# Third part's x and C by seven products, head 0 loaded amid the quads, and a new order at the heads' ends and at SwiGLU's front

## The chip, the cores and the metric

The kernel runs on one core of one Trainium2 chip. Its time is the device time of one execution in microseconds (us). Runs of one kernel differ by about 0.1%: the three runs of before lie between 1023.2 and 1024.15 us. All matrix work is done in fp32 through three products of operands split into a high and a low part, so TensorE (PE) does three matmuls for each product of the reference.

## The reference, cut to what matters

One encoder layer on 512 tokens of width 1024 with 4 heads (query and key width 256, value width 512) and a SwiGLU layer of width 2816:

```python
h    = rmsnorm(x, g_mix)
proj = h @ w_in
xc, gb, gc, q, k, v, g_sw, gate_a, gate_r = split(proj)
u    = gc * xc
y_a  = (gb * dwconv3(u)) @ w_a_out                      # mixer A
ret  = retention(q, k, v)                               # mixer B, both directions
y_r  = (groupnorm_per_head(ret) * swish(g_sw)) @ w_r_out
m    = sigmoid(gate_a) * y_a + sigmoid(gate_r) * y_r
x    = x + m @ w_o
x    = x + swiglu(rmsnorm(x, g_ffn))
y    = rmsnorm(x, g_final)
```

## The kernel before, in words

**Units.** Every weight goes through the core in units of 128x1024 numbers. SyncE (SP) loads a raw unit, ScalarE (ACT) casts it to its high part (L202, names `whi<-raw`), VectorE (DVE) subtracts that for the low part (L203, `wlo<-raw,whi`), and PE multiplies high by high, high by low and low by high. `plan()` lists all units in the order of their use, raw loads go out four steps of the plan ahead, and two units are kept split ahead.

**Two ways to multiply.** A plain block (`feature_major`, L341 to L343) takes 48 matmuls of 512 columns for 256 output features. A quad (`fm_quad` with `prod`, L382; `strassen` with `prod_tm`, L426) makes two such pairs of results, for two column blocks and two halves of the tokens, from 7 products of quarter matrices where the plain way has 8. In `fm_quad` one product is 24 matmuls of 256 columns. Four of the seven weight operands (t1 to t4) are sums of quarters. For most quads DVE adds them (L300). For the quads in the list `SUMMED` they are made in DRAM by copying and accumulating DMAs that GpSimd (POOL) issues (`sum_step`, L264 to L273), one step behind a store or a pow that is named for it.

**Mixer A.** Its 1024 features are done in four parts of 256: for each x, then C (multiplied into u, then the 3-tap convolution on ACT and DVE, L776 and L778), then B (multiplied in, L818 or L845), then the result's forms z are split and stored to DRAM through POOL's queue (`z_forms`). Before, x and C of the parts 0 and 1 are two quads, B of both is a third one, and the parts 2 and 3 are plain blocks (`do_mix(2)`, `do_mix(3)`).

**The heads.** The main sequence after the projection is: `mix_quads()`, `load_head(0)` (query, key, value, gate, decay table), `do_scores(0)` (24 matmuls of 512 columns; their eviction is L872, then hi and lo), `split_v`, `do_mix(2)`. Then for each head: load the next head, `do_pv` (48 matmuls; for each of four token blocks statistics L893 to L895 on DVE, a pow on POOL L896, a multiply on DVE L899, a scaling on ACT L901), scores of the next head, `do_t` (16 transposes on DVE, L217), and a piece of other work for PE behind which these hide: `do_mix(3)` for head 0, the W_r product of the head before (`do_wr`, its sums on DVE are L933) for the others.

**SwiGLU's front.** The last products of m @ W_o add into y (`join`, L1021). `complete` squares a finished half row on ACT (L1026), scales and sums on DVE (L1028, L1031), takes the pow on POOL (L1033) and normalizes on DVE (L1036). `tr_o` transposes the result on PE (L1049), and splits it (ACT L1052, DVE L1054) beside an fp32 copy on ACT (L1053). From these come four forms s1 to s4 (DVE L1002, then split by L202 and L203) that SwiGLU's first quad needs for its second, third, fifth and seventh product. While they are made, PE runs the first products of other quads (`first_tokens`).

The pools that this touches: 14 tiles of 1 MB, 5 units each of high and low parts, 9 tiles of 128x512, 10 raw tiles, 8 banks of PSUM.

Of the kernel before, what the change touches and what calls it, by code (L numbers as in the profile page):

```python
# [17 lines left out]
P = 128  # L18
# [53 lines left out]

def plan():

    out = []  # L80

    def a(name, col):
        out.append(("c", name, 0, 8, col, 256))

    def b(name, row, nk, col, nc):
        out.append(("c", name, row, nk, col, nc))

    def quad(c0, c1):
# [12 lines left out]
    for c in (0, 512):  # L101
        quad(C_GA + c, C_GR + c)
    for c0, c1 in ((C_XC, C_GC), (C_XC + 256, C_GC + 256), (C_GB, C_GB + 256)):
        for name in FORMS:
            out.append(("q", ("x", c0, c1), name, 0, 4))
    for s in (2, 3):
        for c in (C_XC, C_GC, C_GB):
            a("w_in", c + s * 256)
    for h in range(HEADS):
        for c in (0, 512):  # L110
            b("w_r_out", h * VD, 4, c, 512)
    for kind, name in [("a", x) for x in FORMS[:6]] + [("o", "b11"), ("a", "b22")] + [
            ("o", x) for x in ("t1", "t2", "b21", "b22", "t3", "t4")]:
        for u in (0, 2):
            out.append(("q", (kind,), name, u, 2))
    def f(q, *names):
        for n in names:
            out.append(("q", ("f", q), n, 0, 4))

    for q, name in FIRST_PRODUCTS:  # L120
        f(q, name)
    for q0, n in FF_PARTS:
        for q in range(q0, q0 + n):
            between, behind = beside(q)
            f(q, "t1", "t2")
            if between:
                f(*between)
            f(q, "t3")
            if behind:
                f(*behind)  # L130
            f(q, "t4", "b22")
        units = [(name, u) for name in FORMS for u in range(0, n, 2)]
        if q0 + n == NQ:

            i = units.index(("b21", 2))
            units[i:i + 3] = units[i + 1:i + 3] + units[i:i + 1]
        for name, u in units:
            out.append(("q", ("d", q0), name, u, min(2, n - u)))
    return out
# [9 lines left out]
SUMMED = (("f", 0), ("f", 1), ("o",))  # L149
# [24 lines left out]
def block_kernel(ctx: ExitStack, tc: tile.TileContext, xw0, xw, xT, xtok, wpack, wquad, cols, decs, rot, g_ffn, g_final, out):  # L174
# [23 lines left out]

    def split(src, hi, lo, scale=None, round=None):

        if scale is None:
            first = (round or nc.scalar.copy)(hi, src)  # L202
            nc.vector.tensor_tensor(out=lo, in0=src, in1=hi.bitcast(F32), op=ALU.subtract)  # L203
# [18 lines left out]

    made = []
# [7 lines left out]
    def prefetch_block(loads, splits):  # L231
# [4 lines left out]
        for c in range(2):  # L236
            if loads:
                loads(c)
            nc.sync.dma_start(st[c], wpack[i][:, c * QH:(c + 1) * QH])
# [22 lines left out]
    steps = {"quads": sums_of(SUMMED[:2]), "heads": sums_of(SUMMED[2:])}  # L262
# [16 lines left out]

    def load_raws(upto):  # L280
        while loaded[0] < len(LOADS) and LOADS[loaded[0]][0] <= upto:
# [3 lines left out]
            nc.sync.dma_start(t[:, 0:n], src[:, 0:n])  # L285
            raws[quad, name, u] = t
            loaded[0] += 1
# [456 lines left out]
    def do_quad(left, right, func, func_left=None):  # L744
        def ev_sum(dst, o, f):
            def ev(tt, t):
# [3 lines left out]
                if tt and not o:  # L750
# [56 lines left out]
    def do_mix(s):  # L807
        us, c = [], bigtile()[:, 0:2, :]
        feature_major(xg, lambda m, ps: us.append(snap(ps)))
        u = u_tile()  # L810

        def ev_c(m, ps):
            nc.vector.tensor_tensor(out=u[:, m, 1:513], in0=ps, in1=us[m], op=ALU.mult)
            conv(m, 2 * s + m, u[:, m], c[:, m])
        feature_major(xg, ev_c)

        def ev_b(m, ps):
            nc.vector.tensor_tensor(out=c[:, m], in0=ps, in1=c[:, m], op=ALU.mult)  # L818
        feature_major(xg, ev_b)
        z_forms(s, c)  # L820

# [4 lines left out]

    def mix_quads():

        c = bigtile().rearrange("p (s m) t -> p s m t", s=2)
        for s in range(2):  # L830
            u, got = u_tile(), {}

            def ev21(ps):
                nc.vector.tensor_tensor(out=u[:, :, 257:513], in0=halves(ps), in1=halves(got["c2"]), op=ALU.mult)

            def ev12(t):
                nc.vector.tensor_tensor(out=u[:, :, 1:257], in0=halves(got["x1"]), in1=halves(t), op=ALU.mult)
            fm_quad(xf, lambda t: got.update(x1=t), ev21, lambda t: got.update(c2=t), ev12)
            for m in range(2):
                conv(m, 2 * s + m, u[:, m], c[:, s, m])  # L840
# [6 lines left out]
        fm_quad(xf, times(0, T1), times(0, T2), times(1, T2), times(1, T1))  # L847
        for s in range(2):
            z_forms(s, c[:, s])


    def load(src, dt=F32):
        t = bigtile(dt)
        nc.sync.dma_start(t if dt == F32 else t.bitcast(F32), src)
# [28 lines left out]
    def do_pv(p, vv, sg):  # L883

        for nb in range(NB):
# [11 lines left out]
            sum_step(power, "heads")  # L897
# [40 lines left out]
    mix_quads()  # L938
    nxt = load_head(0)
# [61 lines left out]
    def form(out, name, o, in0, in1, op):  # L1001
        nc.vector.tensor_tensor(out=o, in0=in0, in1=in1, op=op)  # L1002
        out[name] = form_tile()
        split(o, *out[name])

# [33 lines left out]
    def tr_o(nb):  # L1039
        th, o = nb // 2, (nb % 2) * P  # L1040
        if nb % 2 == 0:
            t = bigtile()
            for q in range(2):
                XF[q, th] = form_tile()
                xf32[q, th] = t[:, 2 * q:2 * q + 2, :].rearrange("p a (b c) -> p (a b) c", c=256)
        for q in range(2):
# [3 lines left out]
            ps = ps.rearrange("p (k t) -> p k t", k=4)  # L1050
            hi, lo = (t[:, :, o:o + P] for t in XF[q, th])
            nc.scalar.copy(hi, ps)  # L1052
            nc.scalar.copy(xf32[q, th][:, :, o:o + P], ps)  # L1053
            nc.vector.tensor_tensor(out=lo, in0=ps, in1=hi.bitcast(F32), op=ALU.subtract)  # L1054
# [36 lines left out]
    def ev(tt):  # L1091
        join(2 + tt, 1, a[tt], ALU.subtract)
        complete(2 + tt, 1, 0)
        if tt == 0:
            tr_o(0)
    prod_tm(4, of(M["s3"]), a, False, False, ev)

    def ev(tt):
        join(2 + tt, 0, a[tt])
        complete(2 + tt, 0, 1)  # L1100
        if tt == 0:
            tr_o(1)
# [115 lines left out]
    form(XF, "s4", a12, a12, a22, ALU.add)  # L1218
# [179 lines left out]
```

## Time and profile before

| what | before |
|---|---|
| time, median of three runs (lowest, highest) | 1023.71 us (1023.2, 1024.15) |
| the profiled execution, its own time | 1024.53 us |
| its span, first to last instruction | 1022.7 us |
| granted clock of PE | 1.000 |
| busy: POOL | 138.1 us, 14% |
| DMA: over the span | 211 GB/s |

The span leaves 1.8 us of the profiled execution's time that lie around it. A row of a timeline or of the chain of waits gives a start and a length in us, the engine, the line and the names; in brackets behind it stands how long the engine had been idle and what released it. In the groups, the number behind x is a count, then come busy us and the mean of one in ns, then the idle time ahead of them. A matmul's length in the timeline is longer than the distance to the next one's start, because matmuls overlap: the distance is what one costs.

### The profile page before, as it was taken

The page shows a single profiled execution, that of the slowest core. Times are in us where ns is not written, and L with a number is a line of the kernel's source. Part 1 is how long each engine was busy: PE and PEld are TensorE (multiplying, and loading weights), DVE is VectorE, ACT ScalarE, POOL GpSimd, SP SyncE. Part 2 cuts the span into 40 slices and gives each one's busy share as a digit, 9 for nine tenths or more (in the row PEclk, how much of TensorE's full clock was granted, in tenths as well). Part 3 has the DMA queues.
Part 4 walks back from the last instruction along what each step waited for, and adds up shares of the span by engine and source line. Part 5 has one row for each costly group of instructions (what it writes and reads, how often), then busy time and mean ns, then how long its engine had stood idle before and what let it go on. Part 6 is the DMA issues. An engine that isn't in the chain of part 4 may idle for free.

```text
span 1022.7 us, 14808 instructions
## 1 busy us (share of the span) xinstructions
PE 1012.4 (99%) x5586; PEld 882.3 (86%) x5586; DVE 902.7 (88%) x1169; ACT 548.0 (54%) x744; POOL 138.1 (14%) x221
## 2 busy tenths in 40 slices
PE   9999999999999999999999999999999999999997
PEld 7888888888888998888888788889998999899986
DVE  7878998979798988797979898999998999889996
ACT  7547656553656455342532325576654565556554
POOL 0030231222112003304021100010002000110011
PEclk9999999999999999999999999999999999999999
DMA  9525487694767657939496855573418522663433
GB/s 348 208 73 196 167 296 216 206 319 144 258 205 231 257 200 264 347 125 340 116 349 262 261 212 180 153 247 120 140 38 223 179 83 83 192 157 105 165 69 97
DMA packets 53352, 200.24 MB, mean 196 GB/s; under 512 B 7264, under 2 KB 7392, under 8 KB 48672
## 3 DMA queue, kind: packets, MB, share of 16 engines
q1 hardware_dynamic: 37600, 137.39, 38.4%
q0 software_dynamic: 15392, 61.62, 20.8%
q8 instruction: 44, 0.72, 0.3%
q10 hardware_dynamic: 288, 0.29, 0.1%
q14 instruction: 28, 0.23, 0.1%
HBM read 160.73 MB, written 55.31 MB: 211 GB/s over the span
## 4 chain that ended last, share of the span: by engine, by line
PE 41%; DVE 6%; issue 2%; POOL 1%; ACT 1%; DMA 0%; POOLq 0%; DVEq 0%
PE bank L382 21%; PE bank L426 17%; DVE big L217 2%; PE bank L341 1%; DVE big L933 1%; PE bank L342 1%; PE bank L343 1%; DVE wlo L203 1%; DVE big L206 0%; DVE big L203 0%; PE bank L994 0%; POOL bnmv L896 0%; DMA raw<-wquad 0%; PE bank L1049 0%; DVE bnst L893 0%
## 5 line engine op out<-in xcount | busy, mean ns | idle before, releaser
L202 ACT CAST whi<-raw 128x1024 fp32r<-128x1024 f32 (+2 forms) x299 | 302.7, 1028 | 256.6 <-PE bank L426 62.2
L203 DVE TENSOR_TENSOR wlo<-raw,whi 128x1024 fp32r<-128x1024 f32 (+2 forms) x300 | 352.2, 1190 | 64.3 <-ACT whi L202 63.8
L382 PE MATMUL bank<-xform,whi 128*128 128x256 f32 x1424 | 257.8, 283 | 0.9 <-DVE xform L203 0.6
L382 PEld LDWEIGHTS bank<-xform,whi 128*128 128x128 f32 x1424 | 222.1, 192 | 2.2 <-DVE xform L203 0.8
L382 PE MATMUL bank<-xform,wlo 128*128 128x256 f32 x712 | 201.1, 283 | 0.4 <-DVE wlo L203 0.4
L426 PE MATMUL bank<-whi,big 128*128 128x512 f32 x596 | 187.5, 390 | 0.0
L426 PE MATMUL bank<-whi,xform 128*128 128x512 f32 x496 | 157.1, 390 | 0.0
L300 DVE TENSOR_TENSOR raw<-raw 128x1024 f32<-128x1024 f32 (+1 forms) x128 | 151.7, 1201 | 4.9 <-DMA raw<-wquad 4.0
L382 PEld LDWEIGHTS bank<-xform,wlo 128*128 128x128 f32 x712 | 136.4, 192 | 0.6 <-DVE wlo L203 0.6
L426 PEld LDWEIGHTS bank<-whi,big 128*128 128x128 f32 x596 | 111.9, 188 | 24.0 <-ACT t L433 0.4
L426 PE MATMUL bank<-wlo,big 128*128 128x512 f32 x298 | 116.0, 389 | 0.0
L426 PEld LDWEIGHTS bank<-whi,xform 128*128 128x128 f32 x496 | 92.9, 188 | 19.7 <-DVE xform L203 0.6
L426 PE MATMUL bank<-wlo,xform 128*128 128x512 f32 x248 | 96.5, 389 | 0.0
L433 ACT COPY t<-bank 128x512 f32<-128x512 f32 x105 | 61.1, 586 | 56.0 <-PE bank L382 29.7
L341 PE MATMUL bank<-big,whi 128*128 128x512 f32 x220 | 85.7, 390 | 0.0
L343 PE MATMUL bank<-big,wlo 128*128 128x512 f32 x220 | 85.6, 389 | 0.0
L342 PE MATMUL bank<-big,whi 128*128 128x512 f32 x220 | 85.6, 389 | 0.0
L426 PEld LDWEIGHTS bank<-wlo,big 128*128 128x128 f32 x298 | 55.9, 188 | 11.4
L426 PEld LDWEIGHTS bank<-wlo,xform 128*128 128x128 f32 x248 | 46.6, 188 | 9.6
L341 PE MATMUL bank<-whi,big 128*128 128x512 f32 x128 | 49.9, 390 | 1.2 <-DVE big L933 1.2
L342 PE MATMUL bank<-wlo,big 128*128 128x512 f32 x128 | 49.8, 389 | 0.0
L343 PE MATMUL bank<-whi,big 128*128 128x512 f32 x128 | 49.8, 389 | 0.0
(202 smaller groups left out, 1375.1 us busy)
## 6 DMA issues: line engine op xcount, KB each, us to landing
raw<-wquad SPq DMA_DIRECT2D x140, 512.0 KB, 4.9
raw<-wpack SPq DMA_DIRECT2D x42, 512.0 KB, 5.8
t_f<-wquad POOLq DMA_DIRECT2D x12, 512.0 KB, 6.4
z<-t POOLq DMA_DIRECT2D x24, 256.0 KB, 4.5
t_o<-wquad POOLq DMA_DIRECT2D x12, 512.0 KB, 7.8
zform<-z POOLq DMA_DIRECT2D x6, 1024.0 KB, 7.1
v<-t POOLq DMA_DIRECT2D x16, 256.0 KB, 5.5
sg<-t POOLq DMA_DIRECT2D x16, 256.0 KB, 4.9
```

Source lines behind the costliest of these rows:

```text
L202: first = (round or nc.scalar.copy)(hi, src)
L203: nc.vector.tensor_tensor(out=lo, in0=src, in1=hi.bitcast(F32), op=ALU.subtract)
L217: nc.vector.transpose(o[:, :, :, b, :], i[:, :, :, q, :])
L300: nc.vector.tensor_tensor(out=t, in0=t, in1=raws[quad, more, u][:, 0:n], op=ALU.add)
L341: nc.tensor.matmul(ps, lh, rh, start=first, stop=False)
L342: nc.tensor.matmul(ps, lh, rl, start=False, stop=False)
L343: nc.tensor.matmul(ps, ll, rh, start=False, stop=last)
L382: nc.tensor.matmul(o, l[:, c], r[:, k], start=start and s == 0 and k == 0 and i == 0, stop=stop and k == 3 and i == 2, skip_group_check=True)
L426: nc.tensor.matmul(pss[tt], l, r[:, c], start=start and k == 0 and i == 0, stop=stop and k == n - 1 and i == 2, skip_group_check=True)
L433: nc.scalar.copy(t, ps)
L933: nc.vector.tensor_tensor(out=t, in0=ps, in1=t, op=ALU.add)
```

## The change

Five edits, whose line numbers in the rows below are those of the changed kernel where they stand after the word "now":

1. The third part's x and C become a third quad, `xc_quad(2)`, ahead of B's quad. Its sums are made in DRAM (it heads the list `SUMMED`), with eight more DMAs of POOL, so that all 24 steps "quads" are spread over twice as many stores as before. `do_mix(2)` keeps B alone, 48 matmuls. The plan loses two plain blocks (4 units) and gains 7 units.
2. Query, key, value and gate of head 0 are loaded by SP amid the raw loads from the second quad on, one behind every third of them. The decay table follows B's quad. Loads of plain blocks after that stand behind the last head load.
3. In `do_pv`, the four DMAs of the steps "heads" stand behind the head's last pow, not one behind each.
4. `complete`: the factor 1/D moves into the Square, the addition of EPS to POOL, the last sum to ACT. `tr_o`: both transposes first, then hi and lo, and the fp32 copies behind the last lo. `tr_o(0)` is called after the twelfth matmul of its place rather than amid them, and `tr_o(1)` ahead of the last twelve matmuls of W_o.
5. SwiGLU's front: form s2 follows s1 at once, and each further form stands behind the split of the one before.

```diff
+XC = ("x", C_XC + 512, C_GC + 512)
...
-    for c0, c1 in ((C_XC, C_GC), (C_XC + 256, C_GC + 256), (C_GB, C_GB + 256)):
+    for c0, c1 in ((C_XC, C_GC), (C_XC + 256, C_GC + 256), XC[1:], (C_GB, C_GB + 256)):
...
-        for c in (C_XC, C_GC, C_GB):
+        for c in (C_GB,) if s == 2 else (C_XC, C_GC, C_GB):
...
-SUMMED = (("f", 0), ("f", 1), ("o",))
+SUMMED = (XC, ("f", 0), ("f", 1), ("o",))
...
-                if tt and not o:
+                if tt:
                     sum_step(last)
...
     def mix_quads():
...
+        xc_quad(0, c[:, 0])
+        head = []
+        for src, dt in ((qkd[0][0], F32R), (qkd[0][1], F32R), (vd[0], F32), (sgd[0], F32)):
+            among.append(lambda src=src, dt=dt: head.append(load(src, dt)))
+        xc_quad(1, c[:, 1])
+        part2.append(bigtile()[:, 0:2, :])
+        xc_quad(2, part2[0])
...
             power = nc.gpsimd.tensor_tensor(out=mv[:, 3:4], in0=mv[:, 2:3], in1=mhalf[:, 0:1], op=ALU.pow)
-            sum_step(power, "heads")
+            if nb == NB - 1:
+
+                for _ in range(4):
+                    sum_step(power, "heads")
...
-        nc.scalar.activation(t512(), yt, AF.Square, accum_out=ac[:, last:last + 1])
+        nc.scalar.activation(t512(), yt, AF.Square, scale=D ** -0.5, accum_out=ac[:, last:last + 1])
         if not last:
-            nc.vector.tensor_scalar(out=ac[:, 3:4], in0=ac[:, 0:1], scalar1=1.0 / D, scalar2=EPS,
-                                    op0=ALU.mult, op1=ALU.add)
+            nc.gpsimd.tensor_scalar_add(ac[:, 3:4], ac[:, 0:1], EPS)
             return
-        nc.vector.scalar_tensor_tensor(out=ac[:, 4:5], in0=ac[:, 1:2], scalar=1.0 / D,
-                                       in1=ac[:, 3:4], op0=ALU.mult, op1=ALU.add)
+        nc.scalar.activation(ac[:, 4:5], ac[:, 1:2], AF.Identity, bias=ac[:, 3:4])
...
     form(XF, "s1", a22, a21, a22, ALU.subtract)
+    low = form(XF, "s2", a22, a22, a11, ALU.subtract)
     first_tokens(*FIRST_PRODUCTS[2])
-    form(XF, "s2", a22, a22, a11, ALU.subtract)
     first_tokens(*FIRST_PRODUCTS[3])
-    form(XF, "s3", a21, a11, a21, ALU.subtract)
+    with tc.issue_after(low.ins):
+        low = form(XF, "s3", a21, a11, a21, ALU.subtract)
```

Three places where the rows of an engine change. The first is DVE between the scores of head 0 and `do_pv(0)`. Before (t512_3608 is the last block of scores, big_3567 the low part of the scores, big_3613 that of v, in two halves, and u_3685 the product of C and x):

```order
L872 SCALAR_TENSOR_TENSOR t512_3608<-bank_3601,tab_3556 128x512
L203 TENSOR_TENSOR big_3567<-t512_3597,big_3566 128x512
L203 TENSOR_TENSOR big_3613<-big_3562,big_3612 128x1024
L203 TENSOR_TENSOR big_3567<-t512_3608,big_3566 128x512
L203 TENSOR_TENSOR big_3613<-big_3562,big_3612 128x1024
L203 TENSOR_TENSOR wlo_3697<-raw_3689,whi_3696 128x1024
L203 TENSOR_TENSOR wlo_3763<-raw_3758,whi_3762 128x1024
L813 TENSOR_TENSOR u_3685<-bank_3700,t512_3656 128x512
```

Now the same steps (big_3859 is the low part of v), with the multiplications by B (L884) straight behind them:

```order
L911 SCALAR_TENSOR_TENSOR t512_3854<-bank_3847,tab_3750 128x512
L210 TENSOR_TENSOR big_3813<-t512_3843,big_3812 128x512
L210 TENSOR_TENSOR big_3859<-big_3337,big_3858 128x1024
L210 TENSOR_TENSOR big_3813<-t512_3854,big_3812 128x512
L210 TENSOR_TENSOR big_3859<-big_3337,big_3858 128x1024
L884 TENSOR_TENSOR big_3296<-bank_3876,big_3296 128x512
L884 TENSOR_TENSOR big_3296<-bank_3902,big_3296 128x512
L210 TENSOR_TENSOR wlo_4145<-raw_4137,whi_4144 128x1024
```

DVE's own steps up to v's low part stand as before; what has gone is the work with x and C behind it, and on PE the matmuls between the scores and `do_pv(0)` fall from 144 to 48.

The second place is POOL at the end of head 2. Before, pows and DMAs (t2 is the sum in DRAM, first copied from t1, then added to) alternate:

```order
L896 TENSOR_TENSOR bnmv_4602<-bnmv_4602,mhalf_188 128x1
L273 DMA t2_0_o_90<-t1_0_o_89 16x8192
L896 TENSOR_TENSOR bnmv_4624<-bnmv_4624,mhalf_188 128x1
L273 DMA t2_2_o_94<-t1_2_o_93 16x8192
L896 TENSOR_TENSOR bnmv_4646<-bnmv_4646,mhalf_188 128x1
L271 DMA t2_0_o_90<-wquad 64x2048
L896 TENSOR_TENSOR bnmv_4668<-bnmv_4668,mhalf_188 128x1
L271 DMA t2_2_o_94<-wquad 64x2048
```

Now the four pows come first:

```order
L935 TENSOR_TENSOR bnmv_4708<-bnmv_4708,mhalf_192 128x1
L935 TENSOR_TENSOR bnmv_4729<-bnmv_4729,mhalf_192 128x1
L935 TENSOR_TENSOR bnmv_4750<-bnmv_4750,mhalf_192 128x1
L935 TENSOR_TENSOR bnmv_4771<-bnmv_4771,mhalf_192 128x1
L283 DMA t2_0_o_94<-t1_0_o_93 16x8192
L283 DMA t2_2_o_98<-t1_2_o_97 16x8192
L281 DMA t2_0_o_94<-wquad 64x2048
L281 DMA t2_2_o_98<-wquad 64x2048
```

No pow has a DMA ahead of it any more, in head 2 and likewise in head 3.

The third place is DVE at SwiGLU's front. Before, the forms (L1002, in the order s1 to s4) come ahead of the low parts of s2, s3 and s4 (the last three xform rows):

```order
L1002 TENSOR_TENSOR big_6089<-big_6089 128x1024
L203 TENSOR_TENSOR wlo_6200<-raw_5990,whi_6199 128x1024
L1002 TENSOR_TENSOR big_6089<-big_5948,big_6089 128x1024
L203 TENSOR_TENSOR xform_6157<-big_6089,xform_6157 128x1024
L1163 TENSOR_TENSOR t512_6191<-bank_6203,t512_6191 128x512
L1002 TENSOR_TENSOR big_6089<-big_6089,big_5948 128x1024
L203 TENSOR_TENSOR wlo_6236<-raw_6056,whi_6235 128x1024
L1002 TENSOR_TENSOR big_5948<-big_5948,big_6089 128x1024
L203 TENSOR_TENSOR xform_6194<-big_6089,xform_6194 128x1024
L203 TENSOR_TENSOR xform_6230<-big_6089,xform_6230 128x1024
L203 TENSOR_TENSOR xform_6267<-big_5948,xform_6267 128x1024
L203 TENSOR_TENSOR wlo_6274<-raw_6108,whi_6273 128x1024
```

Now each form (L1043) is followed by its own low part and by weight units:

```order
L1043 TENSOR_TENSOR big_6195<-big_6195 128x1024
L1205 TENSOR_TENSOR t512_6301<-bank_6309,t512_6301 128x512
L210 TENSOR_TENSOR wlo_6410<-raw_6270,whi_6409 128x1024
L210 TENSOR_TENSOR xform_6263<-big_6195,xform_6263 128x1024
L1043 TENSOR_TENSOR big_6195<-big_6195,big_6067 128x1024
L210 TENSOR_TENSOR wlo_6442<-raw_6303,whi_6441 128x1024
L210 TENSOR_TENSOR xform_6267<-big_6195,xform_6267 128x1024
L1043 TENSOR_TENSOR big_6195<-big_6067,big_6195 128x1024
L210 TENSOR_TENSOR wlo_6474<-raw_6339,whi_6473 128x1024
L210 TENSOR_TENSOR xform_6336<-big_6195,xform_6336 128x1024
L1043 TENSOR_TENSOR big_6067<-big_6067,big_6195 128x1024
```

The low parts of s1 and s2 move ahead of the forms s3 and s4, and a weight unit stands between every two forms.

More of the change, by code (lines that the diff above doesn't have):

```diff
@@ L1 @@
-from contextlib import ExitStack
+from contextlib import ExitStack, nullcontext
 import numpy as np
@@ L202, in split @@
             first = (round or nc.scalar.copy)(hi, src)
[L203 removed]
+            low_of[0] = nc.vector.tensor_tensor(out=lo, in0=src, in1=hi.bitcast(F32), op=ALU.subtract)
         else:
@@ L221, in block_kernel @@
     block = [0]
+    behind = []
     made = []
@@ L238, in prefetch_block @@
                 loads(c)
-            nc.sync.dma_start(st[c], wpack[i][:, c * QH:(c + 1) * QH])
+            with tc.issue_after(behind[-1].ins) if behind else nullcontext():
+                nc.sync.dma_start(st[c], wpack[i][:, c * QH:(c + 1) * QH])
         for c in range(2):
@@ L284, in load_raws @@
             src = wsum[quad, name, u] if name[0] == "t" else quarter(quad, name, u)
-            nc.sync.dma_start(t[:, 0:n], src[:, 0:n])
+            raw = nc.sync.dma_start(t[:, 0:n], src[:, 0:n])
             raws[quad, name, u] = t
+            if among and loaded[0] % 3 == 0:
+                with tc.issue_after(raw.ins):
+                    among.pop(0)()
             loaded[0] += 1
@@ L847, in mix_quads, with do_mix, ev_c, ev_b @@
         fm_quad(xf, times(0, T1), times(0, T2), times(1, T2), times(1, T1))
+        while among:
+            among.pop(0)()
+        tab = misctile(896, "tab")
+        nc.sync.dma_start(tab, tabs[0])
         for s in range(2):
             z_forms(s, c[:, s])
+        behind.append(last[-1])
+        return head[0:2], tab, *head[2:]
+    def do_mix(s):
+        if s == 2:
+            c = part2[0]
+        else:
+            us, c = [], bigtile()[:, 0:2, :]
+            feature_major(xg, lambda m, ps: us.append(snap(ps)))
+            u = u_tile()
+            def ev_c(m, ps):
+                nc.vector.tensor_tensor(out=u[:, m, 1:513], in0=ps, in1=us[m], op=ALU.mult)
+                conv(m, 2 * s + m, u[:, m], c[:, m])
+            feature_major(xg, ev_c)
+        def ev_b(m, ps):
+            nc.vector.tensor_tensor(out=c[:, m], in0=ps, in1=c[:, m], op=ALU.mult)
+        feature_major(xg, ev_b)
+        z_forms(s, c)
+    last = []
     def load(src, dt=F32):
         t = bigtile(dt)
-        nc.sync.dma_start(t if dt == F32 else t.bitcast(F32), src)
+        last.append(nc.sync.dma_start(t if dt == F32 else t.bitcast(F32), src))
         return t
@@ L1049, in tr_o @@
                 nc.tensor.transpose(ps[:, k * P:(k + 1) * P], hs[nb][q][:, k * P:(k + 1) * P], ident)
[L1050 to L1054, printed above, removed]
+            pss.append(ps.rearrange("p (k t) -> p k t", k=4))
+            last = split(pss[q], *(t[:, :, o:o + P] for t in XF[q, th]))
+        with tc.issue_after(last.ins):
+            for q in range(2):
+                nc.scalar.copy(xf32[q, th][:, :, o:o + P], pss[q])
     po = {}
```

51 lines of the change are left out of this document (22 added, 29 removed).

## The prediction

> **What bounds the kernel now.** I read the page first, for the engine that is full:
>
> ```profile
> PE 1012.4 (99%) x5586; PEld 882.3 (86%) x5586; DVE 902.7 (88%) x1169; ACT 548.0 (54%) x744; POOL 138.1 (14%) x221
> ```
>
> PE is busy for 99% of the span at a granted clock of 1.000, so time goes down by fewer or cheaper matmuls, or by the few places where PE waits. The list of PE's waits names those, with total, count and longest:
>
> ```profile
> PE bank L476 <- DVE t L473: 1.4, 1, 1.4
> PE bank L341 <- DVE big L933: 1.2, 1, 1.2
> PE bank L382 <- DVE xform L203: 0.6, 1, 0.6
> PE bank L382 <- DVE wlo L203: 0.4, 1, 0.4
> PE bank L1049 <- DVE t L1036: 0.3, 1, 0.3
> PE bank L382 <- ACT xform L1052: 0.2, 1, 0.2
> ```
>
> The first is the program's start, which the change leaves. The second is the end of the heads, the other four lie at SwiGLU's front. Together these five are 2.7 us, and as matmuls' starts show below they cost some 4.0. What a matmul costs is read from two undisturbed stretches of the chain of waits (start, length, count):
>
> ```profile
> 602.77 27.20 PE bank L426 x120
> ...
> 709.23 48.73 PE bank L382 x404
> ```
>
> 512 columns cost 27.20/120 = 0.2267 us, 256 columns 48.73/404 = 0.1206 us, a little over half (0.1134).
>
> **The products.** The third part's x and C lose 2 x 48 matmuls of 512 columns, 96 x 0.2267 = 21.76 us, and gain 7 x 24 of 256 columns, 168 x 0.1206 = 20.26 us. PE is full on both sides, so this is -1.5 us. One product in eight is saved, 2.7 us at equal price per column; the shorter matmuls take 1.2 back. The Trainium skill, page "TensorE: Matmul & The Clock Gate", section "Back-to-back issue gap", gives for an isolated matmul N/2.4 + 2.5 ns; by that estimate the edit would bring 20.7 - 18.3 = 2.4 us. The same section gives 131 ns for 512 columns in a stream; by that the 96 old matmuls would take only 12.6 us and the edit would lose. The trace's 0.2267 us in a stream of 120 speaks against the second figure, and its 0.1206 is above the first, so neither enters the sum.
>
> The quad's weights cost DVE 7 subtractions where 4 were, and its evictions a few more; that falls into the stretch before 400 us, where DVE's busy time (third column behind the window: PE, PEld, DVE) stays under PE's:
>
> ```profile
> 360.00:380.00 20.00, 20.00 (x161) 19.42 (x160) 17.47 (x22) 11.30 (x14) 0.03 (x1) 1.00 0.48 172
> 380.00:400.00 20.00, 20.00 (x110) 17.44 (x109) 17.44 (x32) 9.05 (x14) 10.50 (x16) 1.00 0.87 310
> 400.00:420.00 20.00, 20.00 (x90) 16.53 (x89) 12.77 (x18) 7.98 (x11) 0.00 (x0) 1.00 0.79 298
> ...
> 460.00:480.00 20.00, 20.00 (x90) 16.57 (x89) 13.45 (x22) 5.57 (x8) 4.81 (x7) 1.00 0.94 354
> ```
>
> Its four sums come from DRAM, so no L300 additions join. I cost this at nothing; without that cover it would be some 4 us.
>
> **A new wait at head 0's P times V.** Before, DVE splits v behind the scores while PE has 144 matmuls of `do_mix(2)` to do; now there are 48. The scores end where the first matmul from whi starts, and v's low part is the pair of 128x1024 subtractions:
>
> ```profile
> 388.72 0.39 PE L343 MATMUL bank<-big 128*128 128x512 f32 x1
> 388.94 0.39 PE L341 MATMUL bank<-big,whi 128*128 128x512 f32 x1
> ```
> ```profile
> 392.73 0.69 DVE L203 TENSOR_TENSOR t<-t,t 128x512 fp32r<-128x512 f32 x1 [0.82 <-DMA z<-t]
> 394.80 0.69 DVE L203 TENSOR_TENSOR t<-t,t 128x512 fp32r<-128x512 f32 x1 [1.39 <-DMA z<-t]
> ...
> 399.94 1.22 DVE L203 TENSOR_TENSOR big<-big 128x1024 fp32r<-128x1024 f32 x1
> ...
> 401.68 1.22 DVE L203 TENSOR_TENSOR big<-big 128x1024 fp32r<-128x1024 f32 x1
> 402.82 2.36 DVE L203 TENSOR_TENSOR wlo<-raw,whi 128x1024 fp32r<-128x1024 f32 x2
> ```
>
> PE would be through B at 388.94 + 48 x 0.2267 = 399.8. The second matmul of P times V needs v's first low half, done at 401.1 (start plus length), so PE waits some 1.2 us; its eighth needs the second half, done at 402.9, which gives another 0.3. Sum +1.5 us. DVE's order up to there is unchanged, and so is what delays it: two waits, 2.2 us, for z stores to land and free their tiles. If other loads move out of z's way, v is ready at 398.9 and the cost is 0; if they double, it is 3.7. I take 1.5, the rows as they stand. DVE's work with B and z, now bunched behind it, runs out in the loose 460 to 480 window (13.45 of 20).
>
> **The heads' ends.** POOL runs its queue in order. At head 3 the last variance was ready at 561.96, but POOL stood before a DMA that waited for another to land:
>
> ```profile
> 561.81 0.15 DVE L895 TENSOR_SCALAR bnmv<-bnmv 128x1 f32<-128x1 f32 x1
> ...
> 565.97 11.45 DVE L217 STREAM_TRANSPOSE big<-big 32x512 f32<-32x512 f32 x16 [3.34 <-ACT big L901]
> ...
> 581.30 1.28 DVE L933 TENSOR_TENSOR big<-bank,big 128x512 f32<-128x512 f32 x2
> ```
> ```profile
> 563.72 0.86 POOL L271 DMA_DIRECT2D t_o<-wquad  x1 [2.77 <-DMA t_o<-t_o]
> 564.32 0.86 POOL L896 TENSOR_TENSOR bnmv<-bnmv,mhalf 128x1 f32<-128x1 f32 x1
> ```
> ```profile
> 580.48 0.39 PE L343 MATMUL bank<-whi,big 128*128 128x512 f32 x1
> 582.04 0.50 PE L341 MATMUL bank<-whi,big 128*128 128x512 f32 x1 [1.17 <-DVE big L933]
> ```
>
> With the pow first, it starts 564.32 - 561.96 = 2.4 us earlier, and so do the 16 transposes and the sums that release PE. PE's shortfall is 582.04 - 580.48 - 0.23 = 1.33, and 0.1 on the next matmul; it goes as a whole, with 0.9 us to spare: -1.4. The lower end is -1.0, if the transposes gain less than that. The four DMAs now wait behind the pow, POOL alone holds them, and the next things in its queue are form loads that waited for PE until 579.8 anyway. The Trainium skill, page "DMA: Bandwidth & Descriptors", section "Anatomy of one DMA", says that a DMA's wait is done by the issuing sequencer ahead of dispatch; the row of 2.77 us agrees. It also prices a DMA at 2.0 us plus bytes at 436 GB/s, an estimate of 3.2 us for these 512 KB, by which the pow would hardly have waited; the page of the profile has more than twice that, and the sum goes by it:
>
> ```profile
> t_f<-wquad POOLq DMA_DIRECT2D x12, 512.0 KB, 6.4
> z<-t POOLq DMA_DIRECT2D x24, 256.0 KB, 4.5
> t_o<-wquad POOLq DMA_DIRECT2D x12, 512.0 KB, 7.8
> ```
>
> The quad's own eight sums use this queue too. Its last four follow one another where f's came two and two, so a DMA can wait up to 6.4 us less the distance to the one before, and stores to DRAM stand behind it. At the spacing of the stores there that is 0 to 4 us of POOL, which PE sees only if the nine t512 tiles run out: 0, at most 0.5.
>
> **SwiGLU's front.** PE's rows there, each with the one ahead of it:
>
> ```profile
> 676.03 0.39 PE L426 MATMUL bank<-wlo,xform 128*128 128x512 f32 x1
> 676.76 0.63 PE L1049 MATMUL bank<-ident,t 128*128 128x128 f32 x4 [0.34 <-DVE t L1036]
> ...
> 681.32 1.03 PE L1049 MATMUL bank<-ident,t 128*128 128x128 f32 x8
> 682.60 0.39 PE L382 MATMUL bank<-xform,whi 128*128 128x256 f32 x1 [0.24 <-ACT xform L1052]
> ...
> 704.44 0.76 PE L382 MATMUL bank<-xform,whi 128*128 128x256 f32 x5
> 705.83 0.39 PE L382 MATMUL bank<-xform,whi 128*128 128x256 f32 x1 [0.63 <-DVE xform L203]
> ...
> 708.56 0.28 PE L382 MATMUL bank<-xform,wlo 128*128 128x256 f32 x1
> 709.23 0.39 PE L382 MATMUL bank<-xform,wlo 128*128 128x256 f32 x1 [0.39 <-DVE wlo L203]
> ```
>
> Against the steady distances the shortfalls are 0.5 (676.76 - 676.03 - 0.23), 0.5 (682.60 less eight transposes of 0.11, and 0.1 on the next), 0.9 (705.83 less five times 0.12, and 0.1) and 0.65: 2.55 in all. The first two get cover: `tr_o(0)` moves behind four more matmuls (0.9 us), and twelve (2.7 us) follow `tr_o(1)`. The third is s2's low part, which stood behind two forms, s3 and s4, and now stands ahead of them. The fourth is a weight unit behind three low parts in a row, now spread out. DVE's work itself barely falls, so I leave 0.35 of the last: -2.2, between -2.55 and -1.0. EPS on POOL is used only once the second half row is squared, so its price is hidden.
>
> **The sum.** -1.5 + 1.5 - 1.4 - 2.2 = -3.6 us on the profiled execution's 1024.53, which is 1020.9. That execution lies 0.8 above the median of 1023.71; from the median the forecast is 1020.1. All terms at their good ends give -5.5 (1018.2), all at their bad ends -1.5 + 3.7 - 1.0 - 1.0 + 0.5 = +0.7 (1024.4).
>
> **The rivals.** *Nothing new waits, all named waits go*: z's stores land in time and v is ready. For it speaks that the two waits hang on the DMA engines alone (share 0.87 between 380 and 400), where loads run beside z's stores; against it, the order of these loads hardly changes. 1018.2.
>
> *DVE is the bound at the front.* There it works 19.27 of 20 us:
>
> ```profile
> 680.00:700.00 20.00, 19.76 (x151) 18.75 (x150) 19.27 (x29) 16.97 (x30) 2.00 (x2) 1.00 0.50 156
> ```
>
> A PE that arrives 1 us earlier then finds the next unit 1 us late, and only 0.5 of the 2.55 is kept: -1.5 + 1.5 - 1.4 - 0.5 = -1.9, 1021.8. Against it: behind 709.23 PE did not wait again, though four units stood in a row.
>
> *Slower: z's stores hold up head 0.* DVE reaches v only behind two waits for z stores. If these land in 7.8 us, as POOL's accumulating transfers do, and not in 4.5, each wait grows by 3.3 and P times V waits 1.5 + 6.6 = 8.1 us: -1.5 + 8.1 - 1.4 - 2.2 = +3.0, 1026.7. It turns slower by over 0.2% once they need over 7.3 us. Against it: the same stores go out at the same point with no more traffic beside them.
>
> *The seven products are not cheaper*, if the shorter matmuls cost what the 512 do per column and 0.03 us more: 168 x 0.143 = 24, which gives +2.3 in place of -1.5, 1023.9. The x404 row excludes it almost wholly.
>
> **How the numbers follow.** Forecast 0.50, all waits gone 0.17, DVE's bound 0.20, slower through z 0.12, no cheaper products 0.01. About 0.2%, 2.05 us, is what a measurement can tell from no change: faster means under 1021.7, slower over 1025.8. So faster is 0.50 + 0.17 = 0.67, the same 0.20 + 0.01 = 0.21, slower 0.12. The range, 1018.2 to 1024.4, is that of the terms' ends; it leaves out the slower case and some of the tails.
>
> **What would show it.** Right: seven groups of L382-like matmuls more, 168 in 20.3 us; one PE wait of 1 to 1.5 us on DVE's split of v behind B's 48 matmuls; no wait on L933's successor near 577; pow rows at head 3 without a DMA between; the four front waits gone or one small. Wrong: a PE wait of over 4 us at head 0, waits at the front that kept their sum under other names, or a new wait in the quads of 100 to 300 us behind POOL's stores.

## The result, and the profile after

The changed kernel takes 1031.86 us (median of 6 runs, 1030.32 to 1032.42) where the kernel before took 1023.93 beside it (6 runs, 1023.2 to 1025.63): ratio 1.007, 95% interval 1.006 to 1.008. It is slower by 7.9 us. The profiled execution took 1031.72 us with a span of 1029.9 and a mean granted clock of PE of 0.995, not 1.000.

The list of PE's waits after (total, count, longest):

```profile
PE bank L356 <- ACT big L209: 4.3, 1, 4.3
PE bank L357 <- DVE big L210: 2.1, 1, 2.1
PE bank L1090 <- DVE t L1076: 1.6, 1, 1.6
PE bank L491 <- DVE t L488: 1.4, 1, 1.4
```

The waits at head 3 (1.2) and at SwiGLU's forms (0.6 and 0.4) have gone. In their place stand two at head 0's P times V, 6.4 us together, and one of 1.6 ahead of the transposes at SwiGLU's front. The quads themselves came out near what was worked out; the chain of waits has 26 of their products, of 24 matmuls each, in a row:

```profile
323.48 75.65 PE bank L397 x624
```

That is 75.65/624 = 0.1212 us for a matmul of 256 columns, with the short delays at the starts of some products included.

**Head 0.** PE's timeline from the end of B's 48 matmuls:

```profile
421.06 0.39 PE L358 MATMUL bank<-big,wlo 128*128 128x512 f32 x1
425.72 0.59 PE L356 MATMUL bank<-big 128*128 128x512 f32 x1 [4.27 <-ACT big L209]
428.40 0.80 PE L357 MATMUL bank<-big 128*128 128x512 f32 x1 [2.09 <-DVE big L210]
428.99 0.63 PE L358 MATMUL bank<-big 128*128 128x512 f32 x1
429.41 0.63 PE L356 MATMUL bank<-big 128*128 128x512 f32 x1
...
432.82 0.40 PE L358 MATMUL bank<-big 128*128 128x512 f32 x1
```

Beyond the steady 0.227 us from start to start, the first two gaps are 4.4 and 2.45 us. After them PE goes on at 0.43 us a matmul, about half speed, until 432.8: another 2.2 us. Sum 9.1. The table of windows shows the granted clock there (the third number from the end):

```profile
420.00:440.00 20.00, 13.64 (x50) 10.48 (x49) 17.32 (x32) 8.23 (x12) 7.48 (x12) 0.83 0.85 316
```

What PE waited for is on DVE, the rows that answer to the two waits for z stores of before (0.82 and 1.39 us):

```profile
414.05 0.69 DVE L210 TENSOR_TENSOR t<-t,t 128x512 fp32r<-128x512 f32 x1 [0.96 <-DMA z<-t]
420.07 0.69 DVE L210 TENSOR_TENSOR t<-t,t 128x512 fp32r<-128x512 f32 x1 [5.33 <-DMA z<-t]
421.30 0.43 DVE L210 TENSOR_TENSOR t<-big,t 128x256 fp32r<-128x256 f32 x1 [0.53 <-DMA z<-t]
421.64 0.68 DVE L911 SCALAR_TENSOR_TENSOR t<-bank,tab 128x512 f32<-128x512 f32 x1
423.38 1.43 DVE L911 SCALAR_TENSOR_TENSOR t<-bank,tab 128x512 f32<-128x512 f32 x2 [1.05 <-DMA z<-t]
...
427.12 1.22 DVE L210 TENSOR_TENSOR big<-big 128x1024 fp32r<-128x1024 f32 x1
```

Now they are four waits with 7.9 us, and the scores (L911) and the split of v (the last row) stand behind them. The DMA issues from 400 to 425 us say which transfers ran together (KB, median us from issue to landing):

```profile
z<-t POOLq DMA_DIRECT2D x12, 256.0 KB, 8.0
...
big<-qh SPq DMA_DIRECT2D x1, 1024.0 KB, 9.0
big<-ql SPq DMA_DIRECT2D x1, 1024.0 KB, 12.0
big<-v SPq DMA_DIRECT2D x1, 1024.0 KB, 8.0
```

The same view of before, from 380 to 400 us:

```profile
z<-t POOLq DMA_DIRECT2D x12, 256.0 KB, 4.4
```

The z stores take nearly twice as long. The four of 256 KB that go out between 410.4 and 414.9 us take 11.0 us to land; three that go out ahead of them, between 400 and 408, take 5.2. Between the two groups lie the loads of query and key of head 1 (qh holds their high parts, ql the low parts). SP's timeline of the changed kernel has them at 410.62, 4 us after the end of B's quad at 406.5; in the kernel before they stand at 405.75, 21 us after its end at 385.1. The value of head 1 follows only at 421.75, when DVE's longest wait is over:

```profile
410.62 0.33 SPq L893 DMA_DIRECT2D big<-qh  x1
411.11 0.33 SPq L893 DMA_DIRECT2D big<-ql  x1
421.75 0.32 SPq L893 DMA_DIRECT2D big<-v  x1
```
```profile
405.75 0.33 SPq L854 DMA_DIRECT2D big<-qh  x1
```

**SwiGLU's front.** PE's timeline at the new wait:

```profile
694.45 0.28 PE L397 MATMUL bank<-xform,wlo 128*128 128x256 f32 x1
696.34 1.38 PE L1090 MATMUL bank<-ident,t 128*128 128x128 f32 x8 [1.61 <-DVE t L1076]
```

These are the transposes of token block 2. DVE's timeline shows why their input is late: the join of that block (L1063) stands behind the low parts of `tr_o(1)` (the xform row), 3.4 us after PE had finished its product at 688.1:

```profile
690.32 1.29 DVE L210 TENSOR_TENSOR xform<-bank,xform 128x512 fp32r<-128x512 f32 x2
691.52 1.28 DVE L1063 TENSOR_TENSOR big<-big,bank 128x512 f32<-128x512 f32 x2
...
695.53 1.41 DVE L1076 SCALAR_TENSOR_TENSOR t<-big,ac,gb 128x512 f32<-128x512 f32 x2 [0.46 <-POOL ac L1073]
```

**The sum of PE's shortfalls.** For each profile I added up how much later each matmul starts after the one before than the steady distance (0.2267 us for 512 columns, 0.120 for 256, 0.110 for a transpose), by stage. The stages with head 0 and behind are given in us of the span; for the kernel before, head 0's P times V lies at 422 and for the changed kernel at 421:

| kernel | start, to 20 | to 406 | head 0, to 445 | to 570 | to 620 | front, to 730 | rest | steady |
|---|---|---|---|---|---|---|---|---|
| before | 1.5 | 1.6 | 0.0 | 0.0 | 1.5 | 2.9 | 1.2 | 1006.1 |
| changed | 2.2 | 2.1 | 9.1 | 0.0 | 0.0 | 2.7 | 1.1 | 1004.5 |
| late_head1 | 1.9 | 1.8 | 2.7 | 0.5 | 0.0 | 2.7 | 1.0 | 1004.5 |
| z_after | 2.0 | 1.8 | 0.0 | 1.3 | 0.0 | 2.7 | 1.2 | 1004.5 |
| join_first | 1.7 | 1.8 | 8.8 | 0.0 | 0.0 | 2.0 | 1.3 | 1004.5 |
| heads_only | 2.7 | 1.6 | 0.0 | 0.0 | 0.0 | 2.9 | 1.1 | 1006.1 |
| forms_only | 2.2 | 1.6 | 0.0 | 0.0 | 1.6 | 1.6 | 1.3 | 1006.1 |
| no_xc | 1.8 | 1.6 | 0.0 | 0.0 | 0.0 | 1.6 | 1.3 | 1006.1 |
| best | 2.2 | 2.0 | 0.0 | 0.8 | 0.0 | 1.7 | 1.2 | 1004.5 |
| best2 | 2.1 | 1.9 | 0.0 | 0.9 | 0.0 | 1.9 | 3.8 | 1004.5 |

The last column is the sum of all steady distances; it follows from the number of matmuls and is not itself a measurement. From before to changed it falls by 1.6 and the shortfalls rise by 8.6, together +7.0 us; the spans differ by 7.2. The start varies by 1.2 us between executions of whatever kernel, so a single profile's time says nothing about a microsecond, but the stages do.

### The profile page after: what moved, and what is told of

Read it like the earlier page. It is cut to its first block, busy times and chain, and to the rows that moved or that the text cites. A ratio compares the mean times of both kernels' runs of the same rounds, so it can differ in the third digit from the quotient of the medians.

```text
span 1029.9 us, 14988 instructions
## 1 busy us (share of the span) xinstructions
PE 1014.1 (98%) x5658; PEld 886.4 (86%) x5658; DVE 907.3 (88%) x1167; ACT 553.3 (54%) x752; POOL 144.7 (14%) x233
## 4 chain that ended last, share of the span: by engine, by line
PE 91%; DVE 4%; DMA 1%; issue 1%; POOL 1%; ACT 1%; POOLq 0%; DVEq 0%; ACTq 0%
PE bank L441 35%; PE bank L397 29%; PE bank L357 9%; PE bank L356 9%; PE bank L358 9%; DVE wlo L210 1%; DMA z<-t 1%; DVE xform L210 1%; DVE big L1063 1%; POOL z L647 1%; DMA ydr<-big 0%; PE bank L491 0%; DVE big L1043 0%; PE bank L676 0%; DVE big L1017 0%
## 5 line engine op out<-in xcount | busy, mean ns | idle before, releaser
L209 ACT CAST whi<-raw 128x1024 fp32r<-128x1024 f32 (+2 forms) x302 | 306.2, 1029 | 265.9 <-PE bank L441 59.5
L210 DVE TENSOR_TENSOR wlo<-raw,whi 128x1024 fp32r<-128x1024 f32 (+2 forms) x303 | 356.5, 1192 | 66.8 <-ACT whi L209 66.1
L397 PE MATMUL bank<-xform,whi 128*128 128x256 f32 x1488 | 269.3, 283 | 0.0
L397 PEld LDWEIGHTS bank<-xform,whi 128*128 128x128 f32 x1488 | 232.2, 192 | 1.0 <-ACT t L448 0.5
L397 PE MATMUL bank<-xform,wlo 128*128 128x256 f32 x744 | 210.1, 283 | 0.0
L397 PEld LDWEIGHTS bank<-xform,wlo 128*128 128x128 f32 x744 | 142.6, 192 | 0.0
L356 PE MATMUL bank<-big,whi 128*128 128x512 f32 x188 | 73.3, 390 | 0.0
L358 PE MATMUL bank<-big,wlo 128*128 128x512 f32 x188 | 73.2, 389 | 0.0
L357 PE MATMUL bank<-big,whi 128*128 128x512 f32 x188 | 73.1, 389 | 0.0
```

The costliest lines, as they stand in the source:

```text
L210: low_of[0] = nc.vector.tensor_tensor(out=lo, in0=src, in1=hi.bitcast(F32), op=ALU.subtract)
L356: nc.tensor.matmul(ps, lh, rh, start=first, stop=False)
L357: nc.tensor.matmul(ps, lh, rl, start=False, stop=False)
L358: nc.tensor.matmul(ps, ll, rh, start=False, stop=last)
L397: nc.tensor.matmul(o, l[:, c], r[:, k], start=start and s == 0 and k == 0 and i == 0, stop=stop and k == 3 and i == 2, skip_group_check=True)
```

## The experiments

My theory after the result: the loads of head 1 come some 17 us earlier against B's quad than before, take the DMA engines from the z stores, and DVE cannot reach the scores of head 0 until those have landed. The rival: 48 matmuls are too short a cover and POOL's stores are slow by themselves.

**late_head1** holds the four loads of head 1 until the scores of head 0 are split.

```diff
-    def load(src, dt=F32):
+    def load(src, dt=F32, gate=None):
         t = bigtile(dt)
+        if gate is not None:
+            nc.vector.tensor_copy(t[:, 0, 0:1], gate if dt == F32R else gate.bitcast(F32))
...
-        return [load(t, F32R) for t in qkd[h]], tab, load(vd[h]), load(sgd[h])
+        gate = p[1][:, 3, 0:1] if h == 1 else None
+        return [load(t, F32R, gate) for t in qkd[h]], tab, load(vd[h], F32, gate), load(sgd[h], F32, gate)
```

> The changed kernel, with the four loads of head 1 held until the scores of head 0 are split (each load's tile first gets one column written by DVE behind that split). Theory, head 1's loads of 1 MB each collide with the z stores: the z stores land in 4 to 5 us as in the kernel before, DVE's waits for them fall from 7.9 us to 2 to 3, PE waits 1 to 2 us at P times V instead of 4.4 and 2.5, its clock stays at 1.00 there, and the time is 1023.5 to 1025.5 us. Rival, the cover of 48 matmuls is too short and POOL's stores are slow by themselves: waits and time stay within 1.5 us of the changed kernel, 1030.4 or more.

Measured: 1025.03 us beside 1024.45 for the kernel before, ratio 1.0003 (0.9994 to 1.0012), so some 7 us less than the changed kernel. PE's waits and the DMA issues from 400 to 425 us:

```profile
PE bank L1093 <- DVE t L1079: 1.6, 1, 1.6
PE bank L357 <- DVE big L210: 1.5, 1, 1.5
...
PE bank L357 <- DMA big<-ql: 0.2, 1, 0.2
```
```profile
z<-t POOLq DMA_DIRECT2D x12, 256.0 KB, 5.0
```

The theory stands: with nothing changed but the time of these loads, of what stands behind them on SP's queue, and four writes of one column on DVE behind the split, z lands in 5.0 us and not 8.0 (in 5.3 and not 11.0 for the stores sent out between 410.4 and 414.9). DVE waits 2.9 us for it and not 7.9, and PE's first gap is 1.6 us with no half-speed matmuls behind it. The rival holds for those 1.6 us, which is the cost of the short cover. Head 1 then waits a little for its own late loads (the third row).

**z_after** leaves the loads where the change puts them and calls the z forms of part 1 behind the scores and the split of v.

```diff
...
-        for s in range(2):
-            z_forms(s, c[:, s])
+        z_forms(0, c[:, 0])
+        later.append(lambda: z_forms(1, c[:, 1]))
...
     vv, sg = split_v(nxt[2]), nxt[3]
+    later.pop()()
     do_mix(2)
```

> The changed kernel, with the z forms of part 1 called behind the scores and the split of v, so that DVE need not wait for z stores before it reaches them; head 1's loads stay where the change puts them. Theory, the loads only hurt because z's waits stand ahead of the scores on DVE: P times V starts with a wait under 1 us although the z stores still land late, 1021.5 to 1024 us. Rival, DVE's own work or the late loads hold P times V anyway: a PE wait of 3 us or more stays, 1028 or more.

Measured: 1023.81 us, ratio 0.9994 (0.9985 to 1.0003). The waits at P times V are gone altogether, though the loads of head 1 still run beside z (DMA issues from 400 to 425 us):

```profile
big<-ql SPq DMA_DIRECT2D x1, 1024.0 KB, 12.5
```

So the collision costs through the order on DVE: with the scores ahead of the waits, PE is not held. The collision itself is weaker here too, as fewer stores go out together with the loads: one of 256 KB sent out between 410.4 and 414.9 still takes 9.4 us, but the median from 400 to 425 is 5.1. A part of the gain is given back. The P times V of head 2 has to wait for a bank behind the evictions of head 0's W_r product (ACT L973): two starts of PE lie 1.1 us apart, 0.9 more than the steady distance, where the kernel before has no such gap:

```profile
507.57 0.39 PE L358 MATMUL bank<-whi,big 128*128 128x512 f32 x1
508.67 0.50 PE L356 MATMUL bank<-big 128*128 128x512 f32 x1 [0.72 <-ACT big L973]
```

ACT splits the transposed result of head 1 ahead of those evictions, and PE, no longer held at head 0, catches up with them.

**join_first** undoes a part of the fourth edit: the join and the completion of W_o's last products are called ahead of `tr_o(1)`.

```diff
-        if tt == 0:
-            tr_o(1)
         join(2 + tt, 0, a[tt])
         complete(2 + tt, 0, 1)
+        if tt == 0:
+            tr_o(1)
```

> The changed kernel, with the join and completion of W_o's last products called ahead of tr_o(1) again. Theory, the wait of 1.9 us before the transposes of token block 2 comes from that block's join standing behind the low parts of tr_o(1) on DVE: that wait goes, at most 0.5 us comes back at the first product, and the time falls by 1.3 to 2 us, 1030 us. Rival, DVE is full at the front and the wait moves to the next weight unit or form: 1031.5 us or more.

Measured: 1030.36 us beside 1024.45, ratio 1.0057 (1.0043 to 1.0071, 4 runs), which is 5.9 us over the kernel before where the changed kernel is 7.9 over it. The two intervals overlap, so the time alone does not settle it. The trace shows that the wait at the transposes of block 2 falls from 1.6 to 0.5:

```profile
PE bank L1090 <- DVE t L1076: 0.5, 1, 0.5
```

The theory stands for the larger part of this wait. PE's shortfall in the whole stage falls by less, from 2.7 to 2.0, as some 0.4 us come back in small delays at the quad behind it. What still delays the transposes is most likely the pow of that block on POOL, which ends 0.03 us before the normalization that they wait for begins:

```profile
691.98 1.28 POOL L1073 TENSOR_TENSOR ac<-ac,mhalf 128x1 f32<-128x1 f32 x1 [3.96 <-ACT ac L1072]
```

In the kernel before two of the four such pows take 0.54 us. The last section comes back to this; no run takes the delay away.

**heads_only** is the kernel before with the third edit alone.

```diff
-            sum_step(power, "heads")
+            if nb == NB - 1:
+                for _ in range(4):
+                    sum_step(power, "heads")
```

> The kernel before with the third edit alone (the four sums of a head behind its last pow). Forecast: the PE wait of 1.3 us at the sums of head 3 goes and nothing takes its place, 1022.5 us, 0.14% less than before. Rival: PE waits as long a few us later, for the splits of yr or for the loads that are late behind the DMAs, 1023.9 us.

Measured: 1023.94 us beside 1024.45, ratio 0.9993 (0.9984 to 1.0002). The time is the rival's 1023.9, but the interval holds the forecast's ratio, 0.9986, as well as 1: it doesn't tell the gain from nothing. The trace does: the wait on L933 has gone, nothing has come in its place between 445 and 620 us, and the four waits at the front are as before:

```profile
...
PE bank L382 <- DVE xform L203: 0.6, 1, 0.6
PE bank L382 <- DVE wlo L203: 0.4, 1, 0.4
PE bank L1051 <- DVE t L1038: 0.3, 1, 0.3
PE bank L382 <- ACT xform L1054: 0.2, 1, 0.2
```

Its profiled execution lost 1.2 us more at the start than that of before, which hides in these two profiles nearly as much as the edit brings. Why the median of its runs lies only 0.5 us below that of the kernel before is not shown.

**forms_only** is the kernel before with the fifth edit alone.

```diff
...
+    low = form(XF, "s2", a22, a22, a11, ALU.subtract)
     first_tokens(*FIRST_PRODUCTS[2])
-    form(XF, "s2", a22, a22, a11, ALU.subtract)
     first_tokens(*FIRST_PRODUCTS[3])
-    form(XF, "s3", a21, a11, a21, ALU.subtract)
+    with tc.issue_after(low.ins):
+        low = form(XF, "s3", a21, a11, a21, ALU.subtract)
...
-    form(XF, "s4", a12, a12, a22, ALU.add)
+    with tc.issue_after(low.ins):
+        form(XF, "s4", a12, a12, a22, ALU.add)
```

> The kernel before with the fifth edit alone (s2 at once behind s1, each further form behind the split of the one before). Forecast as in the prediction's third and fourth term of the front: the waits of 0.9 and 0.65 us at the first quad's forms and weight unit go, the two at the transposes (0.5 each) stay, PE's shortfall at the front falls from 2.6 to about 1.0 us and the time by 1.5 us, 1022.9 of 1024.4. Rival, DVE is full and the wait only moves: a shortfall of 2.0 us or more at the front, 1024 us or more.

Measured: 1023.37 us beside 1024.92, ratio 0.9985 (0.9976 to 0.9994), and the shortfall between 620 and 730 us falls from 2.9 to 1.6. The two waits at the forms are gone from PE's list, the two at the transposes stand:

```profile
PE bank L343 <- DVE big L935: 1.3, 1, 1.3
PE bank L1052 <- DVE t L1039: 0.3, 1, 0.3
PE bank L384 <- ACT xform L1055: 0.2, 1, 0.2
```

So this edit is worth what was forecast. In the changed kernel its waits are gone as well, and what takes the gain away is the new wait at the transposes of block 2, which join_first puts down, for its larger part, to the fourth edit's order.

**no_xc** has the third and the fifth edit: the kernel before with both diffs above.

> The kernel before with the third and the fifth edit (heads' ends, order of the forms), third part's x and C left as plain blocks. If the two gains of 1.5 us add, PE's shortfall is 0 at head 3 and 1.3 at the front, and the time is 2.9 us below the kernel before, ratio 0.9972. Rival, DVE's backlog at the front eats what the heads gave: ratio 0.9985 as with the fifth edit alone.

Measured: 1022.27 us beside 1024.6, ratio 0.9979 (0.9970 to 0.9988). Of PE's waits three are left, the start's and the two at the transposes:

```profile
PE bank L478 <- DVE t L475: 1.4, 1, 1.4
PE bank L1054 <- DVE t L1041: 0.3, 1, 0.3
PE bank L384 <- ACT xform L1057: 0.2, 1, 0.2
```

The interval holds both the forecast's 0.9972 and the rival's 0.9985, so the time alone doesn't show that the two gains add. The trace does: PE's shortfall is 0.0 between 570 and 620 us and 1.6 at the front, as in the two runs apart. This version beats the kernel before and the changed one.

**best** joins z_after and join_first on the changed kernel, and moves the transposes of block 2 behind one more product.

```diff
     first_tokens(*FIRST_PRODUCTS[0])
-    tr_o(2)
     first_tokens(*FIRST_PRODUCTS[1])
+    tr_o(2)
     tr_o(3)
```

> The changed kernel with the z forms of part 1 behind the scores (as in z_after), the join ahead of tr_o(1) (as in join_first), and both last transposes behind the second product of the front instead of the first. Theory, with the wait at P times V gone and the front's wait covered by one more product of 2.9 us: front's shortfall 0.5 us or less, no wait at head 0, one wait of about 1.3 us at the sums of head 0 where DVE's backlog ends, 1021.5 to 1022.5 us, faster than before by 0.2%. Rival, DVE gives the front's wait back at the forms s1 and s2, which now start later: shortfall 1.5 us or more, 1023.5 us or more.

Measured: 1022.91 us beside 1024.92, ratio 0.9984 (0.9975 to 0.9994), faster than before but less than hoped: the shortfall at the front is 1.7 us. That is the rival's size, but not at the rival's place: 0.8 of it stands at the transposes of block 3, which now follow straight behind and find their input late. The seven products are in this version and not in no_xc, yet it isn't shown to be faster: in the profiles, of their 1.6 us, 0.8 goes between 445 and 570 us, where the evictions of head 0's W_r product stand, and 0.4 in the quads. Its runs also spread more, 1021.1 to 1025.6; whether the loads of head 1 still come in the way in the slower ones is open.

**best2** takes the transposes of block 3 one product further.

```diff
     first_tokens(*FIRST_PRODUCTS[1])
     tr_o(2)
+    first_tokens(*FIRST_PRODUCTS[2])
     tr_o(3)
...
-    first_tokens(*FIRST_PRODUCTS[2])
     first_tokens(*FIRST_PRODUCTS[3])
```

> The kernel best, with the last transposes one product further apart (block 2 behind the second product, block 3 behind the third). Theory: both normalizations are done a product ahead, the front's shortfall falls from 1.4 to 0.5 us or less, and the time is 3.5 us below the kernel before, ratio 0.9966, 0.6 below the kernel without the seven products. Rival: the forms, now starting behind three products, make PE wait 1 us or more at s1 or s2, and the time is that of the kernel best, ratio 0.998.

Measured: 1025.47 us beside 1024.6, ratio 1.0008 (0.9998 to 1.0017). The theory failed. Of the rival, the wait nearly came, 0.8 us on a form's high part; its time didn't, as the ratio is 1.0008 and not 0.998. A new wait of 1.8 us stands far behind the front, where the table has 3.8 us of shortfall and not 1.2:

```profile
PE bank L397 <- ACT whi L209: 1.8, 1, 1.8
...
PE bank L397 <- ACT xform L209: 0.8, 1, 0.8
```

Why the later one, near 787 us, comes from this order is open.

## Why the prediction was wrong, point by point

**The products: right.** Forecast -1.5 us. At the measured 0.1212 us, 168 matmuls cost 20.4 us where the 96 cost 21.8, which is -1.4. From the 200th matmul to the first of head 0's P times V PE takes 374.1 us in the kernel before and 372.8 in z_after, where nothing holds that step. The two rules of the Trainium skill, page "TensorE: Matmul & The Clock Gate", section "Back-to-back issue gap", that were weighed, a gain of 2.4 and a loss, are both off here.

**Head 0's P times V: this step failed.** The prediction priced it at 1.5 us, taking the two z waits as the rows of before had them ("DVE's order up to there is unchanged, and so is what delays it"). Against its slower rival it held that the stores go out "at the same point with no more traffic beside them". The same point is true, against B's quad; no more traffic is not. I had followed the loads of head 0, which the change names, and not those of head 1, which it doesn't: with 96 matmuls of plain blocks gone between B's quad and `load_head(1)`, what stands behind them on SP's queue comes nearer to the quad, and 2 MB fall into the stretch in which the z stores land. (No run tells this apart from the second edit, which also changes the order of SP's loads there.) late_head1 shows both sides. Without the collision PE has a gap of 1.6 us and one of 0.25, close to the 1.2 and 0.3 of the term; with it the step costs 9.1. DVE's waits for z, taken as 2.2 us, were 7.9.

**The rival that came true.** The slower rival had this place and this mechanism, z stores that land in 7.8 us, and had P times V wait 8.1 us in all. They landed in 8.0, and one at the end of the chain in 10.1 (the chain of waits, changed kernel):

```profile
415.15 10.12 DMA z<-t
```

It got a chance of 0.12 since its cause was missing from the profile of before. That its price of 8.1 lies near the 9.1 is in part luck: the gaps were 6.9 us, less than it had, and behind a gap this long PE did not come back at full speed, which it had left out. The 2.2 us of half-speed matmuls follow only where the gaps are 4.4 and 2.45 us; in late_head1, with 1.6, the granted clock of the window stays at 1.00:

```profile
420.00:440.00 20.00, 18.21 (x78) 14.14 (x77) 16.73 (x39) 8.86 (x14) 6.87 (x11) 1.00 0.71 269
```

The Trainium skill says so on the page "TensorE: Matmul & The Clock Gate", section "What's actually happening": after an idle window of about 3.4 us the array's clock falls to half, and returns after as long a stretch of work. The trace agrees in kind: the gap ahead of the fall is 4.3 us, the granted clock is 0.50 in each microsecond from 428 to 432, and the matmuls are back at full speed at 432.8, 4.4 us after the second gap's end.

**The heads' ends: right.** The last pow of head 3 no longer stands behind a DMA of the sums. A load of z forms (L959) does stand between the pows of this head, at 566.61, though "The change" says that no DMA does; it cost nothing, as the variance came later. POOL's timeline has the wait for landing behind it, longer than before and harmless:

```profile
567.90 0.56 POOL L935 TENSOR_TENSOR bnmv<-bnmv,mhalf 128x1 f32<-128x1 f32 x1 [0.72 <-DVE bnmv L934]
568.43 1.03 POOL L283 DMA_DIRECT2D t_o<-t_o  x2
575.34 0.84 POOL L281 DMA_DIRECT2D t_o<-wquad  x1 [5.88 <-DMA t_o<-t_o]
```

PE's shortfall of 1.5 us there is 0.0 in the changed kernel and in heads_only.

**The front: a term that was mis-sized.** Forecast -2.2, measured -0.2 (2.9 to 2.7 in the table). All four named waits went, as forecast, and the gain of the forms is 1.3 in forms_only. What failed is the cover counted for `tr_o(1)`: twelve matmuls behind it for PE, but on DVE its low parts now stand ahead of the join of block 2, which begins the chain to the next transposes. I had priced that move on PE alone. PE loses 2.1 us there now; join_first takes 1.1 of them away.

**The two smaller terms.** The quad's sums on POOL's queue were taken as 0, at most 0.5; the quads lost 0.5 us up to 406 us, at the starts of products, and no wait on POOL's stores shows on PE. EPS on POOL cost nothing that the list of waits shows. DVE's "bound at the front" did not decide: in forms_only and no_xc the order alone removes the waits. The second and the fourth edit were not run by themselves.

## What to carry to other kernels

When work is taken out of PE's path, ask what stood behind it on the queues of the loads: it comes earlier by that much, and what it meets there may be stores for which an engine waits before it reaches the critical step. A step that is moved has to be followed on every engine it has instructions on; on one engine it can be a cover and on another a delay. And a gap of over 4 us on PE cost some 2 us more here, since the matmuls behind it ran at half speed.

## What the runs showed of the hardware that was not expected

Two queues that move data at the same time share the DMA engines closely enough that two 1 MB loads doubled the landing time of the 256 KB stores sent out behind them: 11.0 us in the changed kernel, and 5.3 in late_head1 for those of the same stretch, 410.4 to 414.9 us, with the loads held back. The Trainium skill, page "DMA: Bandwidth & Descriptors", section "SWDGE vs HWDGE vs iDMA", says that the queues of POOL and of SP end in the same engines, which take turns between them; these numbers agree.

The pow of a 128x1 tile on POOL is not of one length: in the changed kernel it took 0.62 us where DVE's subtraction of two operands from SBUF ended 0.2 us after the pow's start, and 1.41 where such a subtraction ran on until 685.62:

```profile
681.81 0.62 POOL L1073 TENSOR_TENSOR ac<-ac,mhalf 128x1 f32<-128x1 f32 x1 [4.34 <-ACT ac L1072]
684.62 1.41 POOL L1073 TENSOR_TENSOR ac<-ac,mhalf 128x1 f32<-128x1 f32 x1 [2.19 <-ACT ac L1072]
```

In six such cases, four in the changed kernel and two in the kernel before, the pow ended 0.40 to 0.43 us behind the end of the subtraction; in the kernel before, two pows beside a DVE operation with one operand from a bank took 0.54. This is a coincidence in time in every case seen, not an experiment. It bears on SwiGLU's front, since the normalization of a block starts behind its pow.
